# Turning the gated rows of two SwiGLU blocks with transposing DMAs instead of TensorE

## The chip, the cores and the metric

The kernel runs on one core of a Trainium2 chip. The metric is the device time of one execution in microseconds. The core's engines each take their instructions in order: TensorE (PE in the profile; its weight loads are PEld), VectorE (DVE), ScalarE (ACT), GpSimd (POOL) and SyncE (SP). An engine that meets an instruction whose input is not there waits, and everything behind it on that engine waits too. DMAs are issued by SP, ACT or POOL and run on 16 DMA engines that all of them share.

## The reference

A decoder layer on 256 tokens with 2048 channels, all in 32-bit floats. The part that the change touches is the SwiGLU block, which occurs twice (in the kernel f1 and f2), each with 5632 hidden channels:

```
def swiglu(x, w_gate, w_up, w_down):
    return (jax.nn.silu(x @ w_gate) * (x @ w_up)) @ w_down

h = h + 0.5 * swiglu(rmsnorm(h, g_ffn1[l]), w1_gate[l], w1_up[l], w1_down[l])
```

Between the two blocks stand a mixer (a gated spatial unit and a windowed attention) and a cross-attention to a memory; a final RMS norm ends the layer.

## The kernel before, in words

**Matrix products.** Each product of two 32-bit matrices is made of three passes of a faster TensorE format. An operand is split into a high part, which ScalarE makes by a cast (L146, tiles ending in h), and a low part, which VectorE makes by subtracting the high part from the original (L147, tiles ending in l). The passes are high by high, low by high and high by low. On top of that, chunks of one kind (S) take seven products of quarter matrices instead of eight, as Strassen and Winograd do, which needs sums of weights: VectorE makes them in three additions (L319, L322, L323, tile t), and ScalarE and VectorE split them too (th, tl). Chunks of kind C and N need no such sums.

**Streaming.** Weights come in chunks of 1 MB, issued by SP into three buffers (f1gw). The split results gwh and gwl have two buffers, the split sums th and tl one. So ScalarE can cast a chunk's weights as soon as TensorE has finished with the chunk two before, and VectorE subtracts behind it.

**The units.** The gate and up projections are made in 11 units per block, 22 in all. A unit is 512 hidden channels, 8 chunks, and takes about 42 us. At its end VectorE puts the seven products together, ScalarE takes the sigmoid-weighted gate (L671, twice, for the two blocks of 128 tokens) and VectorE multiplies gate and up (L675, twice). The results, called the gated rows, are two tiles of 128 tokens by 512 channels, gp and gz (sg in the very first unit).

**Turning.** The down projection contracts over the hidden channels, so the gated rows must be turned: channels to partitions. rows_done (L655) does it. Its generator turns the rows with eight TensorE transposes of 128x128 per unit, by the identity (L230), four into one PSUM bank; ScalarE copies each bank out into the tile a (L665). These pieces of work are laid between the matmuls of the next unit: side_step counts groups of six matmuls, and the generator asks to go on five groups later and then two groups later. When a tile of a is there, acts holds it, and inner (L681) splits it, for the down projection only, long after.

**What sets the order.** TensorE's order is the program's. The other engines' order is chosen by a scheduler when the program is built. The list later holds functions that are called a given number of chunks after they are put in: an entry with 0 is called in the same chunk step, with 2 two steps later.

Of the kernel before, what the change touches and what calls it, by code (L numbers as in the profile page):

```python
# [7 lines left out]

F32 = mybir.dt.float32
F32R = mybir.dt.float32r  # L10
AF = mybir.ActivationFunctionType
ALU = mybir.AluOpType
AX = mybir.AxisListType

P = 128
T = 256
TB = 2
# [15 lines left out]
def layer_kernel(  # L33
# [22 lines left out]
    nc = tc.nc  # L56
# [13 lines left out]
    def nm(s):  # L70
        uid[0] += 1
        return f"{s}_{uid[0]}"

    def m4(s):
        return mid.tile([P, 1024], F32, tag="m4", name=nm(s))

    def s2(s):
        return tmp.tile([P, 512], F32, tag="s2", name=nm(s))

    def bank(s):  # L80
        return trp.tile([P, 512], F32, tag="tr", name=nm(s))
# [8 lines left out]
    def silu_table():  # L90
        t = tiny.tile([P, 1], F32, tag="warmed", name=nm("warmed"))
        return nc.scalar.activation(t, ones[:, :1], AF.Silu)

# [24 lines left out]
    h = const.tile([P, TB, D], F32, name="h")  # L118
# [15 lines left out]
    def square_into(parts_ap, src, width):  # L134
        junk = s2("junk")
        nc.scalar.activation(junk[:, :width], src, AF.Square, accum_out=parts_ap)

    def split_scaled(hi, lo, src, g):

        nc.scalar.activation(hi, src, AF.Copy, scale=g)  # L140
        nc.vector.scalar_tensor_tensor(
# [27 lines left out]
    def form(s):  # L169
        return [fp.tile([P, 4, P], F32R, tag=t, name=nm(s + t)) for t in ("fh", "fl")]  # L170

    class Pair:
        def __init__(self, s, kind, base=None):
            self.kind = kind
            self.base = base or form(s)
            if kind in "SD":
                self.sums = form(s)
                if kind == "D":
                    self.more = [
                        const.tile([P, 2, P], F32R, tag="more" + t, name=nm(s + "more")) for t in "hl"  # L180
                    ]
# [40 lines left out]
    def laid(kind, k, tb):  # L222
        return BASE[kind].index(f"A{tb + 1}{k + 1}")

    def transposed(s, kind, src):

        ps = bank(s).rearrange("p (k t) -> p k t", k=4)
        for k in range(2):
            for tb in range(TB):
                nc.tensor.transpose(ps[:, laid(kind, k, tb), :], src(tb, k), ident)  # L230
        return ps

    def row_tile(kind, v, k):

        return v[:, k::2, :] if kind == "C" else v[:, 2 * k:2 * k + 2, :]

    def pair_from_rows(s, kind, src, gcol):
# [4 lines left out]
        for k in range(2):  # L242
# [4 lines left out]
            else:  # L247
                nc.scalar.activation(row_tile(kind, raw, k), row_tile(kind, ps, k), AF.Copy, scale=g)
        if kind != "N":
# [60 lines left out]
    def load(s, w, kind, pieces, between):  # L310

        raw = stream.tile([P, 4, 512], F32, tag="raw", name=nm(s + "w"), bufs=3)
        wh = stream.tile([P, 4, 512], F32R, tag="wh", name=nm(s + "wh"))
        wl = stream.tile([P, 4, 512], F32R, tag="wl", name=nm(s + "wl"))
        b = {name: (wh[:, i, :], wl[:, i, :]) for name, i in SLOT.items()}
        if kind == "S":
# [9 lines left out]
            for i, names in enumerate((("T1", "T3"), ("T2", "T4"))):  # L326
                th, tl = [
                    stream.tile([P, 2, 512], F32R, tag=f"{n}{i}", name=nm(s + n), bufs=1)
                    for n in ("th", "tl")
# [93 lines left out]
    def side_add(gen):  # L423
        side.append([now[0], gen])
# [33 lines left out]
    later = []  # L458
# [55 lines left out]
    def narrow_unit(s, w, pairs, late, beside):  # L514

        ps = []
        for c in range(2):
            raw = stream.tile([P, 8, 256], F32, tag="raw", name=nm(s + "w"), bufs=3)
            wh = stream.tile([P, 8, 256], F32R, tag="wh", name=nm(s + "wh"))
            wl = stream.tile([P, 8, 256], F32R, tag="wl", name=nm(s + "wl"))  # L520
# [33 lines left out]
    KINDS_D = "NNSNSNSN" + "NSNSNSN" + "NNSNSNN"  # L554
# [41 lines left out]
    def adds(s, c, j0, on_block=None):  # L596
# [10 lines left out]
        def early(u):  # L607
            p1, v, z = s2(s + "p1"), s2(s + "v"), s2(s + "z")
            nc.scalar.activation(p1, u["P1"], AF.Copy, scale=c)
            nc.vector.scalar_tensor_tensor(  # L610
# [40 lines left out]
    def ffn(s, get, rs, wgu, wd, on_block, first=None, on_token_block=None):  # L651
        acts = [None] * 22
        pairs = [None] * 22

        def rows_done(c, rows_):  # L655
            a = m4(s + "a").rearrange("p (q k t) -> p q k t", q=2, k=4)

            def work():
                for q in range(2):
                    yield 5 if q == 0 else 2  # L660
                    ps = transposed(
                        s + "a", KINDS_D[2 * c + q],
                        lambda tb, k: rows_[tb][:, (2 * q + k) * P:(2 * q + k + 1) * P],
                    )
                    nc.scalar.copy(a[:, q], ps)  # L665
                    acts[2 * c + q] = a[:, q]

            side_add(work())

        def gated(up, sg, r, tb):  # L670
            nc.scalar.activation(  # L671
                sg[1], sg[0], AF.Silu, scale=1.0 if r is None else r[:, tb:tb + 1]
            )
# [13 lines left out]
        def gu_unit(c):  # L687
            got = {}

            def late(u):  # L690
                r = rs()
                c22 = s2(s + "u")
                at = {(0, 0): got["p1"], (1, 1): c22, (0, 1): got["v"], (1, 0): got["z"]}
                seven_late(u, got, lambda tb, j: at[tb, j])
                gated(at[0, 1], (at[0, 0], at[0, 0]), r, 0)
                gated(c22, (at[1, 0], at[1, 0]), r, 1)
                rows_done(c, (at[0, 0], at[1, 0]))

            kinds = MORE if 2 <= c <= 9 else FEWER
            order = range(8)  # L700
            if c == (first is not None):
                order = ORDER[first is None]
            u = Unit(s + "g", "".join(kinds[j] for j in order))
            for i in range(8):
                push(
                    u, i, wgu[order[i], c], lambda j=order[i]: get(j),
                    lambda i=i: (
                        i == u.kinds.rindex("S") and seven_early(u, got), i == 7 and late(u)
                    ),
                    beside=lambda i: (  # L710
                        first[2](8 + i) if first is not None and c == 1
                        else rs() if (c, i) == (0, 5) else inner(i - 5) if c == 10 and i >= 5 else None
                    ),
                )

        def plain_gu_unit(c):
            pairs_, before, prep, rs0 = first
            u = Unit(s + "g", "N" * 8, alone=(7,))
            u.gate_first = True

            def late():
                r = rs0()
                sg = [s2(s + "sg") for _ in range(TB)]
                for tb, (g, up) in enumerate((("P2", "Q3"), ("Q4", "R"))):
                    gated(u[up], (u[g], sg[tb]), r, tb)
                rows_done(c, sg)

            pieces = {0: (1, 0, 3, 2), 1: (1, 3, 0, 2)}
            for i in range(8):
                push(  # L730
                    u, i, wgu[i, c], lambda i=i: have(pairs_, i), late if i == 7 else None,
                    pieces=pieces.get(i), beside=prep, before=before,
                )
# [747 lines left out]
```

## Time and profile before

| what | value |
|---|---|
| median of 3 runs | 2049.84 us (2049.66 to 2049.85) |
| span of the profiled execution | 2047.2 us |
| PE busy | 2034.8 us, 99% |
| DVE busy | 1859.5 us, 91% |
| ACT busy | 1225.4 us, 60% |
| DMA, mean | 196 GB/s |
| granted TensorE clock | 0.999 |

The span runs from the first to the last instruction of one profiled execution; the runs' median is 2.6 us more than it, and that difference is taken as fixed. Busy time of an engine counts its instructions, not its DMA issues. A row of the timeline view gives start, duration, engine, line, output and input tile, and in brackets the idle time before it and what ended it.

### The profile page before, as it was taken

What the parts mean: (1) busy time and instruction counts of PE and PEld (TensorE: products, weight loads), DVE (VectorE), ACT (ScalarE), POOL (GpSimd) and SP (SyncE); (2) the same over time, 40 slices, a digit from 0 to 9 for tenths busy, and PEclk for the clock granted to TensorE, in tenths of its full rate; (3) what the DMA queues carried; (4) which work ended last, traced back from release to release, by engine and by line L of the source; (5) the groups of instructions that cost most, each with busy time, mean ns of one, the idle gap of its engine ahead of it and who ended that gap; (6) DMA issues with size and microseconds to landing.
All of it is one profiled execution on the core that took longest, in us unless ns stands there. A gap on an engine that the chain in (4) does not pass through costs nothing.

```text
span 2047.2 us, 24505 instructions
## 1 busy us (share of the span) xinstructions
PE 2034.8 (99%) x9411; PEld 1690.0 (83%) x9411; DVE 1859.5 (91%) x1998; ACT 1225.4 (60%) x1344; POOL 36.6 (2%) x57
## 2 busy tenths in 40 slices
PE   9999999999999999999999999999999999999998
PEld 7888888888888888888888888888888888888886
DVE  6999999999998978988988977899999999999988
ACT  7755555565555766655556665675555556565554
POOL 0000000000000110100000000000000000000000
PEclk9999999999999999999999999999999999999999
DMA  8555555555555565545545544455455555555563
GB/s 312 182 207 204 206 206 185 205 209 192 203 204 203 188 241 178 195 162 185 202 169 186 204 150 155 171 195 214 185 206 202 205 193 206 202 203 209 185 224 126
DMA packets 60421, 402.21 MB, mean 196 GB/s; under 512 B 6912, under 2 KB 8976, under 8 KB 13200
## 3 DMA queue, kind: packets, MB, share of 16 engines
q1 hardware_dynamic: 57856, 393.50, 53.0%
q0 software_dynamic: 2016, 6.30, 0.9%
q8 instruction: 74, 1.21, 0.2%
q10 hardware_dynamic: 432, 0.84, 0.1%
q14 instruction: 43, 0.35, 0.1%
HBM read 398.52 MB, written 2.10 MB: 196 GB/s over the span
## 4 chain that ended last, share of the span: by engine, by line
PE 97%; DVE 1%; ACT 1%; issue 0%; DMA 0%; POOL 0%; POOLq 0%; DVEq 0%; SPq 0%
PE f1gQ L410 16%; PE f2gQ L410 15%; PE f2dQ L410 6%; PE f1dQ L410 6%; PE f1gP L410 6%; PE f2gP L410 6%; PE xqQ L410 3%; PE f2dP L410 3%; PE f1dP L410 3%; PE woQ L410 2%; PE xoQ L410 2%; PE f2dR L410 2%; PE f1dR L410 2%; PE vQ L410 2%; PE mv0Q L410 2%; PE mv1Q L410 2%
## 5 line engine op out<-in xcount | busy, mean ns | idle before, releaser
L147 DVE TENSOR_TENSOR f1gwl<-f1gw,f1gwh 128x1536 fp32r<-128x1536 f32 (+2 forms) x94 | 181.7, 1935 | 19.8 <-ACT f1gwh L146 16.0
L146 ACT CAST f2gwh<-f2gw 128x1536 fp32r<-128x1536 f32 (+1 forms) x88 | 150.7, 1712 | 69.0 <-PE f2gQ L410 45.5
L146 ACT CAST f1gwh<-f1gw 128x1536 fp32r<-128x1536 f32 (+2 forms) x94 | 153.0, 1629 | 59.9 <-PE f1gQ L410 39.0
L147 DVE TENSOR_TENSOR f2gwl<-f2gw,f2gwh 128x1536 fp32r<-128x1536 f32 (+1 forms) x88 | 179.4, 2039 | 9.5 <-ACT f2gwh L146 7.8
L146 ACT CAST f2gth<-f2gt 128x1024 fp32r<-128x1024 f32 x82 | 84.9, 1050 | 75.9 <-DVE f2gt L319 28.8
L146 ACT CAST f1gth<-f1gt 128x1024 fp32r<-128x1024 f32 x76 | 79.0, 1051 | 76.1 <-DVE f1gt L319 30.1
L410 PE MATMUL f2gQ<-f2gwh,n4fh 128*128 128x512 f32 x317 | 124.5, 393 | 0.0
L410 PE MATMUL f2gQ<-f2gwh,n4fl 128*128 128x512 f32 x317 | 123.4, 389 | 0.0
L146 ACT CAST f2dwh<-f2dw 128x2048 fp32r<-128x2048 f32 (+1 forms) x44 | 77.3, 1757 | 61.6 <-PE f2dQ L410 39.6
L410 PE MATMUL f1gQ<-f1gwh,n1fh 128*128 128x512 f32 x286 | 112.4, 393 | 0.0
L410 PE MATMUL f1gQ<-f1gwh,n1fl 128*128 128x512 f32 x286 | 111.3, 389 | 0.0
L146 ACT CAST f1dwh<-f1dw 128x2048 fp32r<-128x2048 f32 (+1 forms) x44 | 77.3, 1758 | 56.6 <-PE f1dQ L410 38.1
L147 DVE TENSOR_TENSOR f2gtl<-f2gt,f2gth 128x1024 fp32r<-128x1024 f32 x82 | 99.6, 1220 | 8.9 <-ACT f2gth L146 8.4
L147 DVE TENSOR_TENSOR f1dwl<-f1dw,f1dwh 128x2048 fp32r<-128x2048 f32 (+1 forms) x44 | 92.1, 2093 | 12.6 <-ACT f1dwh L146 12.5
L147 DVE TENSOR_TENSOR f2dwl<-f2dw,f2dwh 128x2048 fp32r<-128x2048 f32 (+1 forms) x44 | 92.1, 2094 | 11.5 <-ACT f2dwh L146 11.3
L147 DVE TENSOR_TENSOR f1gtl<-f1gt,f1gth 128x1024 fp32r<-128x1024 f32 x76 | 92.4, 1220 | 7.7 <-ACT f1gth L146 7.2
L410 PE MATMUL f2gQ<-f2gwl,n4fh 128*128 128x512 f32 x317 | 97.6, 392 | 0.0
L410 PE MATMUL f1gQ<-f1gwl,n1fh 128*128 128x512 f32 x286 | 88.0, 393 | 0.0
L410 PEld LDWEIGHTS f2gQ<-f2gwh,n4fh 128*128 128x128 f32 x317 | 59.5, 188 | 12.3 <-DVE f2gv L569 0.4
L410 PEld LDWEIGHTS f2gQ<-f2gwh,n4fl 128*128 128x128 f32 x317 | 59.5, 188 | 11.9
L410 PE MATMUL f2gP<-f2gwh,n4fh 128*128 128x512 f32 x176 | 68.8, 391 | 0.0
L410 PEld LDWEIGHTS f2gQ<-f2gwl,n4fh 128*128 128x128 f32 x317 | 58.8, 188 | 12.0
(828 smaller groups left out, 6045.8 us busy)
## 6 DMA issues: line engine op xcount, KB each, us to landing
f2gw<-in_w_gu SPq DMA_DIRECT2D x88, 1024.0 KB, 4.8
f1gw<-in_w_gu SPq DMA_DIRECT2D x86, 1024.0 KB, 4.9
f1dw<-in_w_down SPq DMA_DIRECT2D x44, 1024.0 KB, 4.8
f2dw<-in_w_down SPq DMA_DIRECT2D x44, 1024.0 KB, 4.8
wow<-in_w_out SPq DMA_DIRECT2D x16, 1024.0 KB, 4.8
xqw<-in_w_xq SPq DMA_DIRECT2D x16, 1024.0 KB, 4.8
xow<-in_w_xo SPq DMA_DIRECT2D x16, 1024.0 KB, 4.8
qw<-in_w_in SPq DMA_DIRECT2D x8, 1024.0 KB, 4.8
```

The costliest lines, as they stand in the source:

```text
L146: nc.scalar.copy(hi, src)
L147: nc.vector.tensor_tensor(lo, src, hi.bitcast(F32), ALU.subtract)
L410: nc.tensor.matmul(self.banks[name], x, y, start=name not in self.begun, stop=self.left[name] == 0)
```

## The change

The eight transposes and two copies of each unit go. In their place, each of the two row tiles (512 words of 32 bits in each partition) is seen as 1024 halves of 16 bits. ScalarE copies the halves into a new tile w, first all low halves, then all high halves, two runs without gaps (L664 of the changed kernel, two per unit). ScalarE's queue then issues a transposing DMA from w to a tile t (L669, two per unit): eight blocks of 128x128 of 16 bits, each turned. Four ScalarE copies (L677) put the halves together again as 32-bit words in the tile a, two of them for each tile t. The function turned (parting and issuing) is called in the chunk step in which the rows are finished, joined (the four copies) two steps later. The new tiles w and t are taken from the same pool of six buffers (s2) from which gp, gz and the other row tiles come.

```diff
         def rows_done(c, rows_):
-            a = m4(s + "a").rearrange("p (q k t) -> p q k t", q=2, k=4)
-
-            def work():
+            a = m4(s + "a")
+            words = a.bitcast(U16).rearrange("p (q i t h) -> p q i t h", q=2, i=4, h=2)
+            halves_ = []
+
+            def turned():
+                for tb in range(TB):
+                    w = s2(s + "w").bitcast(U16)
+                    nc.scalar.copy(
+                        w.rearrange("p (h c) -> p h c", h=2),
+                        rows_[tb].bitcast(U16).rearrange("p (c h) -> p h c", h=2),
+                    )
+                    t = s2(s + "t").bitcast(U16)
+                    nc.scalar.dma_start_transpose(t.rearrange("p (b r) -> p b r", b=8), w)
+                    halves_.append(t.rearrange("p (h b t) -> p b t h", h=2, b=4))
+
+            def joined():
                 for q in range(2):
-                    yield 5 if q == 0 else 2
-                    ps = transposed(
-                        s + "a", KINDS_D[2 * c + q],
-                        lambda tb, k: rows_[tb][:, (2 * q + k) * P:(2 * q + k + 1) * P],
+                    kind = KINDS_D[2 * c + q]
+                    for tb in range(TB):
+                        i, j = laid(kind, 0, tb), laid(kind, 1, tb)
+                        nc.scalar.copy(
+                            words[:, q, i:j + 1:j - i], halves_[tb][:, 2 * q:2 * q + 2]
+                        )
+                    acts[2 * c + q] = a[:, q * 512:(q + 1) * 512].rearrange(
+                        "p (k t) -> p k t", k=4
                     )
-                    nc.scalar.copy(a[:, q], ps)
-                    acts[2 * c + q] = a[:, q]
-
-            side_add(work())
+
+            later.append((0, turned))
+            later.append((2, joined))
```

Lines of the changed kernel are 1 later than those of the kernel before ahead of rows_done and 17 later behind it.

**Where the instructions now stand.** On ScalarE, in the kernel before, the stretch from the second gate function of the seventh unit of f1 (f1gz) on. L146 casts weights (gwh) and sums of weights (gth); L665 empties the two banks of turned rows:

```order
L671 ACTIVATE f1gp_460_2459<-f1gp_460_2459 128x512
L146 CAST f1gwh_2519<-f1gw_2518 128x2048
L671 ACTIVATE f1gz_2461<-f1gz_2461 128x512
L146 CAST f1gwh_2553<-f1gw_2552 128x1536
L146 CAST f1gth_2562<-f1gt_2556 128x1024
L146 CAST f1gwh_2601<-f1gw_2600 128x2048
L665 COPY f1a_2517<-f1a_2588 128x512
L146 CAST f1gth_2566<-f1gt_2556 128x1024
L665 COPY f1a_2517<-f1a_2612 128x512
L146 CAST f1gwh_2634<-f1gw_2633 128x1536
```

The two copies stand apart, each between casts. In the changed kernel the same stretch, from the cast behind that gate function on, where L664 parts a row tile, L669 issues its transposing DMA and L677 joins:

```order
L147 CAST f1gwh_2527<-f1gw_2526 128x2048
L688 ACTIVATE f1gz_2461<-f1gz_2461 128x512
L147 CAST f1gwh_2561<-f1gw_2560 128x1536
L664 COPY f1w_2518<-f1gp_472_2459 128x1024
L669 DMA_TRANSPOSE f1t_2520<-f1w_2518 128x8x128
L664 COPY f1w_2522<-f1gz_2461 128x1024
L669 DMA_TRANSPOSE f1t_2524<-f1w_2522 128x8x128
L677 COPY f1a_2517<-f1t_2520 128x2x256
L147 CAST f1gth_2570<-f1gt_2564 128x1024
L677 COPY f1a_2517<-f1t_2520 128x2x256
L677 COPY f1a_2517<-f1t_2524 128x2x256 x2
L147 CAST f1gwh_2607<-f1gw_2606 128x2048
```

All parting, issuing and joining of the unit now stands in one block, with a single cast (gth) in it, between the cast of the next S chunk's weights and the cast of the chunk after it.

On VectorE, in the kernel before, the same place: L675 finishes the gated rows, L319 to L323 add weights, and L147 makes the low parts:

```order
L147 TENSOR_TENSOR f1gwl_2520<-f1gw_2518,f1gwh_2519 128x2048
L675 TENSOR_TENSOR f1gp_460_2459<-f1gv_2460,f1gp_460_2459 128x512
L675 TENSOR_TENSOR f1gz_2461<-f1u_2507,f1gz_2461 128x512
L319 TENSOR_TENSOR f1gt_2556<-f1gw_2552 128x1024
L147 TENSOR_TENSOR f1gwl_2554<-f1gw_2552,f1gwh_2553 128x1536
L322 TENSOR_TENSOR f1gt_2556<-f1gt_2556,f1gw_2552 128x512
L147 TENSOR_TENSOR f1gtl_2563<-f1gt_2556,f1gth_2562 128x1024
L323 TENSOR_TENSOR f1gt_2556<-f1gt_2556,f1gw_2552 128x512
L147 TENSOR_TENSOR f1gwl_2602<-f1gw_2600,f1gwh_2601 128x2048
L147 TENSOR_TENSOR f1gtl_2567<-f1gt_2556,f1gth_2566 128x1024
```

And in the changed kernel:

```order
L692 TENSOR_TENSOR f1gp_472_2459<-f1gv_2460,f1gp_472_2459 128x512
L692 TENSOR_TENSOR f1gz_2461<-f1u_2507,f1gz_2461 128x512
L148 TENSOR_TENSOR f1gwl_2528<-f1gw_2526,f1gwh_2527 128x2048
L320 TENSOR_TENSOR f1gt_2564<-f1gw_2560 128x1024
L148 TENSOR_TENSOR f1gwl_2562<-f1gw_2560,f1gwh_2561 128x1536
L323 TENSOR_TENSOR f1gt_2564<-f1gt_2564,f1gw_2560 128x512
L148 TENSOR_TENSOR f1gtl_2571<-f1gt_2564,f1gth_2570 128x1024
L324 TENSOR_TENSOR f1gt_2564<-f1gt_2564,f1gw_2560 128x512
L148 TENSOR_TENSOR f1gwl_2608<-f1gw_2606,f1gwh_2607 128x2048
L148 TENSOR_TENSOR f1gtl_2575<-f1gt_2564,f1gth_2574 128x1024
```

VectorE has the same work. The two products that finish the gated rows (L692 here) have moved ahead of one low part of 2048 columns; the rows behind it are in the same order. The last four of them, gtl, an addition, gwl and gtl, need the casts gth, gwh and gth that stand in and behind ScalarE's block.

1 line of the change is left out of this document (added).

## The prediction

> **What bounds the kernel now.** I read the page first: its span, the shares of the engines, and the chain that ended last.
>
> ```profile
> span 2047.2 us, 24505 instructions
> PE 2034.8 (99%) x9411; PEld 1690.0 (83%) x9411; DVE 1859.5 (91%) x1998; ACT 1225.4 (60%) x1344; POOL 36.6 (2%) x57
> PE 97%; DVE 1%; ACT 1%; issue 0%; DMA 0%; POOL 0%; POOLq 0%; DVEq 0%; SPq 0%
> ```
>
> TensorE bounds the whole. Whatever leaves its stream is time, if nothing else holds it up. Then I read stretches of 42 us, the length of one unit, in f1 and in f2:
>
> ```profile
> core 0: us, PE busy (x) PEld busy (x) DVE busy (x) ACT busy (x) POOL busy (x), PEclk, DMA share, GB/s
> 274.00:316.00 42.00, 42.00 (x190) 34.76 (x189) 40.26 (x39) 24.38 (x22) 0.00 (x0) 1.00 0.55 200
> 1572.00:1614.00 42.00, 42.00 (x190) 34.76 (x189) 40.39 (x38) 24.45 (x22) 0.00 (x0) 1.00 0.55 204
> ```
>
> This is where the change sits, and 91% is the wrong number here: VectorE is busy 40.3 of 42 us, and has 1.7 us to lose. ScalarE has 17.6 us free, but it is the engine that feeds both.
>
> **What leaves TensorE.** In the chain of waits, between 300 and 325 us, one unit's eight transposes are two pieces:
>
> ```profile
> 314.81 0.44 PE f1a L230 x4
> 318.01 0.43 PE f1a L230 x4
> ```
>
> 0.87 us a unit, on the chain. (The 272 ns that a transpose lasts overlap with its neighbours and are not its price.) 22 units make 19.1 us; that is all that can be won, and the profiled execution would become 2028.
>
> **What ScalarE gets.** Its timeline at the end of f1's seventh unit and in the one that follows:
>
> ```profile
> 297.66 1.48 ACT L146 CAST f1gwh<-f1gw 128x1536 fp32r<-128x1536 f32 x1 [0.59 <-PE f1gQ L410]
> 299.05 1.99 ACT L146 CAST f1gth<-f1gt 128x1024 fp32r<-128x1024 f32 x2
> 307.63 0.63 ACT L671 ACTIVATE f1gz<-f1gz 128x512 f32<-128x512 f32 x1
> 308.16 1.47 ACT L146 CAST f1gwh<-f1gw 128x1536 fp32r<-128x1536 f32 x1
> 312.51 1.06 ACT L146 CAST f1gth<-f1gt 128x1024 fp32r<-128x1024 f32 x1 [2.88 <-DVE f1gt L319]
> 314.43 1.91 ACT L146 CAST f1gwh<-f1gw 128x2048 fp32r<-128x2048 f32 x1 [0.86 <-PE f1gQ L410]
> 316.25 0.58 ACT L665 COPY f1a<-f1a 128x512 f32<-128x512 f32 x1
> 316.72 1.06 ACT L146 CAST f1gth<-f1gt 128x1024 fp32r<-128x1024 f32 x1
> 318.49 0.59 ACT L665 COPY f1a<-f1a 128x512 f32<-128x512 f32 x1 [0.71 <-PE f1a L230]
> ```
>
> Two copies go, 1.17 us. Two partings of 1024 elements come, and four joins of 512. A 16-bit copy is not in this trace; the nearest rows are the cast of 1024 (1.06 us) and the copy of 512 (0.58 us; the next instruction starts after 0.47), and I take these. Bounds: half of it, if an element of half the size takes half the time; twice the parting, if reading every second half costs double. Issue of a DMA by ScalarE, and the time from issue to landing, stand in these rows:
>
> ```profile
> L1400 ACTq DMA_DIRECT2D out<-hg x2: 344/351/358, 2038.8 to 2041.6; - x2
> out<-hg ACTq DMA_DIRECT2D x1, 256.0 KB, 3.2
> mr<-in_mem POOLq DMA_DIRECT2D x8, 256.0 KB, 5.3
> sm<-in_small ACTq DMA_DIRECT2D x1, 52.0 KB, 2.5
> h<-in_x SPq DMA_DIRECT2D x4, 512.0 KB, 10.9
> ```
>
> An issue takes 0.35 us. **The landing time L of a transposing DMA of 256 KB is the unknown of this forecast.** Of the two plain 256 KB transfers the one at the kernel's end, with no load of weights beside it, took 3.2 us, the other, beside such loads, 5.3. The DMA engines are 55% busy here, so I take the middle, 4.25 us. Below, 2.5 us (the smallest transfer on this queue); above, 10.9 us, the slowest row, for the case that eight blocks are turned one after another.
>
> The Trainium skill states two things that disagree. "Advanced Engine Details and Errata", X-Bar Transpose (TRN2), says that transposing DMAs are as fast as plain ones, 350 to 400 GB/s; with the fixed 2.0 us of "DMA: Bandwidth & Descriptors", Anatomy of one DMA, that is an estimate of 2.75 us, and the sum below would give 2059. "VectorE: DVE Perf Modes", The three transpose paths, gives 1309 ns for one 128x128 block by DMA and advises TensorE where PSUM will do; eight blocks in a row would be an estimate of 10.5 us, and 2206. No run here shows which holds yet.
>
> **Where it lands in the program.** Parting, issuing and joining stand in one block on ScalarE behind the cast of 308.16, as the order shows, and the join of the first tile waits for its landing with the casts gth, gwh and gth queued behind it. By the rows above: first parting 309.55 (1.39 behind the cast's start, as from 297.66 to 299.05) to 310.60, issue at 310.60; second parting 310.95 to 312.0, issue to 312.35. First join at 310.60 + L, 314.85 with L = 4.25. Then, at the distances of the trace (0.47 a join, as from 316.25 to 316.72; 0.95 the cast, since two in a row take 1.99 with the overlap), gth at 315.32, a join at 316.27, and the second tile's two at 316.74 and 317.21 (landed at 316.25). The cast gwh starts at 317.68, not 314.43: **late by L - 1.0, 3.25 us**. In general it is the first join, not ScalarE's own work, that sets this as long as L is over 1.75.
>
> **Who waits for it.** VectorE, and then TensorE:
>
> ```profile
> 314.59 1.22 DVE L147 TENSOR_TENSOR f1gtl<-f1gt,f1gth 128x1024 fp32r<-128x1024 f32 x1
> 315.73 0.69 DVE L323 TENSOR_TENSOR f1gt<-f1gt,f1gw 128x512 f32<-128x512 f32 x1
> 316.72 2.29 DVE L147 TENSOR_TENSOR f1gwl<-f1gw,f1gwh 128x2048 fp32r<-128x2048 f32 x1 [0.31 <-ACT f1gwh L146]
> 318.93 1.22 DVE L147 TENSOR_TENSOR f1gtl<-f1gt,f1gth 128x1024 fp32r<-128x1024 f32 x1
> 320.60 0.39 PE L410 MATMUL f1gQ<-f1gth,n1fl 128*128 128x512 f32 x1
> 320.83 1.07 PE L410 MATMUL f1gQ<-f1gtl,n1fh 128*128 128x512 f32 x4
> ```
>
> VectorE's gwl already starts right behind the cast (0.31 idle), and the second gtl right behind gwl. So both move by the same 3.25 us: the second gtl ends at 323.40, not 320.15. TensorE reads it in the third of the four matmuls that begin at 320.83, at 321.28 (a matmul starts every 0.227 us). The slack was 1.13 us. The four transposes of 314.81 and those of 318.01 fall away ahead of that matmul, so it only comes earlier; their 0.87 us is won and lost in the same wait. Per unit the change is
>
> lateness - slack = (L - 1.0) - 1.13 = L - 2.13, at L = 4.25: **+2.12 us**.
>
> VectorE's own account agrees: it can lose 1.7 us a unit; 40.3 of work, with the two new waits ahead of gtl and gwl, 1.8 us each by the same rows, come to 43.9 instead of 41.9.
>
> **The sum.** The chunk order that this rests on (an S chunk, then a C chunk) follows 8 units of each block, 16 in all. The other 6, at the blocks' ends, stand ahead of chunks without that tight gtl; they lie between -0.87 and +2.12, and I take the middle, +0.62. Together 16 x 2.12 + 6 x 0.62 = 37.6 us. In general 19 x (L - 2.13) - 2.6. On the profiled execution 2047.2 becomes 2084.8; on the median, 2.6 us above it, 2049.8 becomes **2088**. With parting at twice the time, 1.05 us more a unit, 2108.
>
> Costed at nothing: the fewer PSUM banks, since no transpose waited for one; the tiles w and t from a pool of six, since each is freed by the joins long before the next unit's rows are made (without that cover the next unit's first copy out of P1 would wait for the joins); and 0.5 MB of transposes beside 8 MB of weights a unit, which SP issues ahead of use into three buffers (if the DMA engines were held for long, the casts would wait for weights).
>
> **The rivals.**
>
> *A transposing DMA lands as a plain one does*, L = 3.2: 19 x 1.07 - 2.6 = +18, **2068**. For it: the same bytes, and the row of this very queue. Against it: that row had the DMA engines to itself. The Trainium skill's first rule is on this side.
>
> *Block after block*, L = 10.9: 19 x 8.77 - 2.6 = +164, **2214**. For it only that 16 bits are moved one by one instead of rows of kilobytes; no row shows it. The Trainium skill's second rule is on this side.
>
> *Faster: the block on ScalarE is short enough.* It wins where the cast gwh is late by less than the slack of 1.13 us; there the wait turns into a part of the 0.87 us. With 16-bit copies at half the time and L = 3.2, the first parting ends at 310.10, the first join starts at 313.30, and gwh at 315.25: late by 0.82, -0.31 a unit. With full copies and a landing that is over before the second issue is, joins start at 312.35 and gwh at 315.18: late by 0.75, -0.38 a unit. With 16 such units and 6 halfway to -0.87 that is -8.5 to -10 us, **2040**. Both at once would win the 19 us, 2031. For it: ScalarE is idle 17.6 of 42 us. Against it: the smallest transfer on its queue needs 2.5 us, and L must be under 2.27 to break even at full copies.
>
> That the transposes stay on TensorE is excluded: none of the 176 stands in its new order.
>
> **How the numbers follow.** My forecast, a landing of 3.6 to 6.5 us, has 0.44 (2075 to 2130 by the formula); the plain landing, 2.4 to 3.6 us (2052 to 2075), 0.21; block after block 0.13; the faster rival 0.22. The time is that of the forecast, 2088. The range takes in the faster rival's two simple forms at 2040 and reaches to a landing of 6.7 us, 19 x 4.57 - 2.6 = +84, 2135 rounded up; what it leaves out is most of the slow case and the best of the faster one. A measurement of this kernel tells 0.2%, 4.1 us, from no change. Of the faster rival 0.18 lies beyond that and 0.04 within, and of the plain landing 0.02 within: faster 0.18, same 0.06, slower 0.76.
>
> **What would show it.** In the changed profile, waits of L677 for a DMA of 1 to 4 us in nearly every unit; the cast gwh behind it 2 to 4 us later against the second gate function; VectorE idle ahead of gtl and gwl for casts; TensorE's idle before matmuls that read gtl, about 2 us a unit, where it had none; a unit of 44 us instead of 41.9. Wrong is the forecast if L677 does not wait, or if it waits and TensorE still has no idle time, because the slack of one chunk was larger than this one unit shows; wrong in size if the issue itself holds ScalarE for microseconds, or if TensorE waits for weights instead.

## The result

The changed kernel takes **2142.62 us** (2141.70 to 2143.80), the kernel before, on the same chip, 2049.76 us: a ratio of 1.0454, with a 95% interval of 1.0441 to 1.0467. It is slower, by 92.9 us. The forecast was 2088 us with a range of 2040 to 2135; the direction was right, and the size was less than half of what came.

The page of the changed kernel, its span and the shares of the engines:

```profile
span 2140.6 us, 24260 instructions
PE 2061.3 (96%) x9235; PEld 1698.1 (79%) x9235; DVE 1860.9 (87%) x1998; ACT 1294.7 (60%) x1432; POOL 34.4 (2%) x57
```

The 176 transposes are gone (9411 to 9235 instructions on TensorE), and yet TensorE is busy 26.5 us longer than before. The span grew by 93.4 us, and these rows split it: TensorE's idle time went from 12.4 us (2047.2 less 2034.8) to 79.3 (2140.6 less 2061.3), which is 66.9 of it; its busy time gives the other 26.5.

Who waits for whom (total us, times, longest), from the view of waits of the changed kernel:

```profile
DVE f1gwl L148 <- ACT f1gwh L147: 68.9, 27, 5.2
...
ACT f1a L677 <- DMA f1t<-f1w: 36.6, 17, 3.9
ACT f2a L677 <- DMA f2t<-f2w: 33.1, 16, 2.9
...
PE f1gQ L411 <- ACT f1gth L147: 31.7, 8, 4.8
...
PE f2gQ L411 <- ACT f2gth L147: 28.5, 7, 4.7
```

The joins wait for the landing; behind them the casts are late, VectorE waits for the cast gwh, and in 15 units, 8 in f1 and 7 in f2, TensorE waits for the cast gth for about 4 us. One such place, on ScalarE:

```profile
291.48 1.47 ACT L147 CAST f1gwh<-f1gw 128x1536 fp32r<-128x1536 f32 x1
292.85 1.04 ACT L664 COPY f1w<-f1gp 128x1024 uint16<-128x1024 uint16 x1
293.92 1.25 ACTq L669 DMA_TRANSPOSE f1t<-f1w  x1
295.21 1.05 ACT L664 COPY f1w<-f1gz 128x1024 uint16<-128x1024 uint16 x1 [1.32 <-issue]
296.29 1.25 ACTq L669 DMA_TRANSPOSE f1t<-f1w  x1
297.58 0.68 ACT L677 COPY f1a<-f1t 128x512 uint16<-128x512 uint16 x1 [1.32 <-DMA f1t<-f1w]
298.17 1.05 ACT L147 CAST f1gth<-f1gt 128x1024 fp32r<-128x1024 f32 x1
299.11 0.68 ACT L677 COPY f1a<-f1t 128x512 uint16<-128x512 uint16 x1
302.12 1.25 ACT L677 COPY f1a<-f1t 128x512 uint16<-128x512 uint16 x2 [2.33 <-DMA f1t<-f1w]
303.28 1.89 ACT L147 CAST f1gwh<-f1gw 128x2048 fp32r<-128x2048 f32 x1
305.08 1.04 ACT L147 CAST f1gth<-f1gt 128x1024 fp32r<-128x1024 f32 x1
```

This is the block that the prediction laid out, with the joins' waits in it (rows of a queue, such as ACTq, are issues). The issue of one DMA holds ScalarE for 1.25 us, the second tile lands 5.8 us after its issue (296.29 to 302.12), and the cast gwh starts 11.80 us after the cast of 1536 columns that leads the block, where it was 6.27 before (308.16 to 314.43). What TensorE does meanwhile:

```profile
302.04 0.39 PE L411 MATMUL f1gQ<-f1gth,n1fl 128*128 128x512 f32 x1
306.17 0.79 PE L411 MATMUL f1gQ<-f1gth,n1fh 128*128 128x512 f32 x1 [3.74 <-ACT f1gth L147]
306.76 0.63 PE L411 MATMUL f1gQ<-f1gth,n1fl 128*128 128x512 f32 x1
307.19 0.63 PE L411 MATMUL f1gQ<-f1gth,n1fh 128*128 128x512 f32 x1
```

It waits 3.74 us, and then its matmuls start 0.43 us apart instead of 0.227. The granted clock says why; stretches of the same execution (PE busy, weight loads, DVE, ACT, POOL, granted clock, DMA share, GB/s):

```profile
305.10:311.90 6.80, 5.73 (x14) 4.35 (x15) 6.66 (x5) 2.75 (x4) 0.00 (x0) 0.50 0.50 177
311.90:352.80 40.90, 38.07 (x168) 31.16 (x166) 33.47 (x33) 24.41 (x23) 0.00 (x0) 1.00 0.60 188
```

**After each of the 15 long waits the clock stands at half for 6.8 us.** In the first of these stretches TensorE was busy 5.73 us for work that needs 2.87 at the full clock. The trace's record of the clock has 15 such stretches, all of 6.83 us; 15 x 2.87 is 43 us. Before, none is in it. (Every kernel's record ends with one more stretch, which begins behind TensorE's last matmul and costs nothing; it is left out here and below.) Another row gives nearly the same: the kernel without the DMAs (no_dma, below) runs the same 9235 instructions of TensorE without a long wait, and its TensorE is busy 2017.3 us; 2061.3 less that is 44.0. So the 93.4 us are +66.9 of idle time, +44.0 of matmuls (some 43 of it at half clock), and -17.5 for the transposes that are gone (2017.3 less 2034.8).

"TensorE: Matmul & The Clock Gate" of the Trainium skill (What's actually happening) says that TensorE falls to half its clock after at least one idle window of about 3.4 us and comes back after a busy one. The halving is in the rows above, and the lengths agree: 6.83 us is two such windows. But no window here had to be idle from end to end, as the trace's record of the clock shows.

**What halves the clock.** In the change the slow stretches begin at 113.93, 161.72 and so on to 448.44 us in f1, and at 1540.70 in f2: 1426.77 us after the first, which is 418 times 3.4133 us. All 51 slow stretches, in the change and the six kernels below that have any, begin on such a grid of fixed moments, one for each execution, to within 5 ns. Cut along it, TensorE's busy time separates all cases: the clock fell after every 3.41-us window at full clock in which TensorE was idle for 1.83 us or more, and after none with less, in all 14 traces. (The least idle time that a fall followed is 1.832 us, the most that none followed 1.828.) It came back after the first window at half clock with less than 0.50 us of idle time. Three windows of the grid, the first two from the change, the third from one_more_copy below (columns as above):

```profile
301.67:305.08 3.41, 0.76 (x4) 0.30 (x2) 0.00 (x0) 2.96 (x3) 0.00 (x0) 1.00 0.81 259
1496.33:1499.74 3.41, 1.60 (x7) 1.32 (x8) 1.62 (x1) 3.41 (x3) 0.00 (x0) 1.00 0.12 50
```

```profile
538.01:541.42 3.41, 1.47 (x8) 0.89 (x6) 1.85 (x4) 3.41 (x5) 0.00 (x0) 1.00 0.29 118
```

The first, with 2.65 us idle, ends where the stretch at half clock above begins, 1.1 us before the wait is over. The second holds nearly all of a wait of 1.89 us, 1.81 us of idle time, and no slow stretch follows; the third holds a whole wait of 1.94 us, and one does.

### The profile page after: what moved, and what is told of

It reads as the page before. It is cut to its first block, busy times and chain, and to the rows that moved or that the text cites. A ratio compares the mean times of both kernels' runs of the same rounds, so it can differ in the third digit from the quotient of the medians.

```text
span 2140.6 us, 24260 instructions
## 1 busy us (share of the span) xinstructions
PE 2061.3 (96%) x9235; PEld 1698.1 (79%) x9235; DVE 1860.9 (87%) x1998; ACT 1294.7 (60%) x1432; POOL 34.4 (2%) x57
## 5 line engine op out<-in xcount | busy, mean ns | idle before, releaser
L147 ACT CAST f1gwh<-f1gw 128x1536 fp32r<-128x1536 f32 (+2 forms) x94 | 152.6, 1625 | 47.4 <-PE f1gQ L411 24.0
L147 ACT CAST f2gwh<-f2gw 128x1536 fp32r<-128x1536 f32 (+1 forms) x88 | 150.0, 1708 | 44.8 <-PE f2gQ L411 28.0
L147 ACT CAST f2gth<-f2gt 128x1024 fp32r<-128x1024 f32 x82 | 85.7, 1050 | 93.3 <-DVE f2gt L320 56.3
L147 ACT CAST f1gth<-f1gt 128x1024 fp32r<-128x1024 f32 x76 | 79.7, 1051 | 90.3 <-DVE f1gt L320 60.6
L147 ACT CAST f2dwh<-f2dw 128x2048 fp32r<-128x2048 f32 (+1 forms) x44 | 77.3, 1757 | 59.2 <-PE f2dQ L411 41.7
L147 ACT CAST f1dwh<-f1dw 128x2048 fp32r<-128x2048 f32 (+1 forms) x44 | 77.2, 1755 | 51.1 <-PE f1dQ L411 33.1
L411 PE MATMUL f2gQ<-f2gth,n4fh 128*128 128x512 f32 x164 | 68.3, 417 | 28.5 <-ACT f2gth L147 28.5
L411 PE MATMUL f1gQ<-f1gth,n1fh 128*128 128x512 f32 x152 | 64.4, 424 | 31.9 <-ACT f1gth L147 31.7
```

What stands on the lines that cost most here:

```text
L147: nc.scalar.copy(hi, src)
L411: nc.tensor.matmul(self.banks[name], x, y, start=name not in self.begun, stop=self.left[name] == 0)
```

## The experiments

Each kernel is the changed one with the edit shown; each ratio is to the kernel before on the same chip, which took 2049.1 to 2049.4 us.

### Taking the DMAs away, and taking only the wait for them away

no_dma leaves the transposing DMAs out and joins the parted rows unturned:

```diff
-                    t = s2(s + "t").bitcast(U16)
-                    nc.scalar.dma_start_transpose(t.rearrange("p (b r) -> p b r", b=8), w)
-                    halves_.append(t.rearrange("p (h b t) -> p b t h", h=2, b=4))
+                    halves_.append(w.rearrange("p (h b t) -> p b t h", h=2, b=4))
```

> As the run whose joins don't wait, and without the DMAs: ScalarE only parts and joins (the down projections get rows that are not turned). Theory: partings and joins together put the second gth cast where it was before, 8.5 us behind the cast of the S chunk's weights; no idle, no half clock: 2031 us, 2028 to 2040; the difference to the run with unawaited DMAs is the price of two issues of 1.25 us. Rival (3.3 us more copying a unit on ScalarE are themselves too much for a VectorE that is 96% busy): over 2055.

Measured: 2033.91 us, 0.9924 (0.9909 to 0.9939). The shares of its engines, from its page:

```profile
PE 2017.3 (99%) x9235; PEld 1672.3 (82%) x9235; DVE 1859.0 (91%) x1998; ACT 1292.9 (64%) x1432; POOL 34.3 (2%) x57
```

TensorE's busy time is the 2017.3 us used above, and it has no wait over 2.2 us. joins_dont_wait keeps both DMAs on ScalarE's queue, but its joins read w, so nobody waits for the landing (rows unturned again):

```diff
-                    halves_.append(t.rearrange("p (h b t) -> p b t h", h=2, b=4))
+                    halves_.append(w.rearrange("p (h b t) -> p b t h", h=2, b=4))
```

> The changed kernel, but the joins read the parted tile w instead of the turned tile t: the DMAs are issued and run, nobody waits for their landing (the down projections get rows that are not turned). Theory (the landing of the second DMA, 5.8 us behind its issue in the unit looked at, is the larger part of the lateness): second gth cast 2.5 us later than in the kernel before instead of 5.0, TensorE idle 1.3 us a unit, shorter than what halves the clock, 2040 to 2065 us. Rival (the issue hold and the copies alone do it): idle of 3 us or more a unit stays, clock 0.50 in nearly every unit, over 2110.

Measured: 2062.60 us, 1.0065 (1.0050 to 1.0080). So the steps from before to the change are -15.2 us for partings and joins in place of TensorE's transposes, +28.7 for having the DMAs issued by ScalarE, and +80.0 for waiting for their landing. They are not quite pure, because the scheduler's order is not the same in the three kernels. On ScalarE all four joins stand ahead of the cast gth in no_dma, and only one of them in the other two, in joins_dont_wait even ahead of the second issue; VectorE's order is the same in nearly all units of f1, but in f2 no_dma has another. Of joins_dont_wait, ScalarE's timeline behind the second issue, and TensorE's waits:

```profile
276.32 1.25 ACTq L669 DMA_TRANSPOSE f1t<-f1w  x1
277.66 1.05 ACT L147 CAST f1gth<-f1gt 128x1024 fp32r<-128x1024 f32 x1 [0.78 <-ACT f1a L677]
```

```profile
PE f2gQ L411 <- ACT f2gth L147: 6.3, 5, 2.4
PE f1gQ L411 <- ACT f1gth L147: 5.6, 7, 0.8
```

The cast gth waits for ScalarE's own issue to be over. The profile names the copy ahead of the issue as what ended its wait, but that copy had long been done. The waits of TensorE are mostly under 1 us, those for gtl (12.2 us in all) included, and the clock stays up: the one wait of 2.42 us was followed by the only slow stretch, of 3.41 us.

### Moving the issue to SyncE's queue alone

sp_alone:

```diff
-                    nc.scalar.dma_start_transpose(t.rearrange("p (b r) -> p b r", b=8), w)
+                    nc.sync.dma_start_transpose(t.rearrange("p (b r) -> p b r", b=8), w)
```

> The changed kernel with its transposing DMAs issued from SP, and the joins where the scheduler puts them, ahead of the casts. Theory: two holds of 1.25 us fall away, the wait for the second landing stays; the second gth cast is about 3.8 us late instead of 5.0, TensorE's idle 2.6 us a unit, too short to halve the clock; 2060 to 2090 us, few or no slow stretches. Rival (the length of the idle does not decide on the clock): slow stretches in nearly every unit and over 2100.

Measured: 2053.59 us, 1.0026 (1.0015 to 1.0036), below what was expected. The issuing queue is the whole edit, and 89 us are gone. The waits of ScalarE's joins, and TensorE's longest:

```profile
ACT f1a L677 <- DMA f1t<-f1w: 20.1, 9, 3.8
...
ACT f2a L677 <- DMA f2t<-f2w: 9.9, 9, 1.2
```

```profile
PE f1gQ L411 <- ACT f1gth L147: 8.8, 8, 2.4
```

The joins still wait, 30.0 us instead of 69.7, but TensorE's longest wait for a gth is 2.4 us, and there are two slow stretches instead of 15 (in the profiled execution, which at 2058.4 us was the slowest of seven). The one edit changes two things: ScalarE is no longer held, and the landing is sooner (median 3.2 us, in the change 3.5 and 4.3); this run doesn't part them. Still, neither waiting for the landing alone nor the issue on ScalarE alone makes the 93 us. Together they bring TensorE's wait to about 4 us, and there each wait has 2.9 us of slow matmuls behind it.

### A plain DMA in its place

plain_dma moves w to t by a plain DMA on the same queue; the rows aren't turned:

```diff
-                    nc.scalar.dma_start_transpose(t.rearrange("p (b r) -> p b r", b=8), w)
+                    nc.scalar.dma_start(t, w)
```

> The changed kernel with a plain DMA from w to t in place of the transposing one, from the same queue (the down projections get rows that are not turned). If a transposing DMA is as fast as a plain one: the same idle times, the same clock, over 2120 us. If the transposing itself costs (issue 1.25 instead of 0.35 us, landing 3.5 to 5.8 instead of some 3.2): idle of about 1 us a unit, no slow stretch, 2040 to 2065 us.

Measured: 2111.52 us, 1.0302 (1.0275 to 1.0330; two runs, 12 us apart), between the two outcomes expected, so neither was right. The time from issue to landing (last number, median us), first of plain_dma, then of the change:

```profile
f1t<-f1w ACTq DMA_DIRECT2D x22, 256.0 KB, 2.5
f2t<-f2w ACTq DMA_DIRECT2D x22, 256.0 KB, 2.4
```

```profile
f1t<-f1w ACTq DMA_TRANSPOSE x22, 3.5
f2t<-f2w ACTq DMA_TRANSPOSE x22, 4.3
```

The plain copy lands 1 to 2 us sooner and its issue takes 0.47 us instead of 1.25. TensorE's waits shrink from about 4 us to between 2.9 and 3.8, and that does not get it out of the trap: 14 waits, 13 slow stretches, nine of 6.83 us and four of 3.41. A wait of 3 us is long enough for the half clock here.

### A later cast in the same trap

one_more_copy puts one more copy of 512 columns on ScalarE ahead of the joins:

```diff
+                nc.scalar.copy(s2(s + "x"), rows_[1])
```

> The changed kernel with one more ScalarE copy of 512 words behind the second issue, whose result nobody reads; by the order, three joins instead of two now stand behind the landing of the second DMA, so the second gth cast starts about 0.57 us later. Theory that the units are locked to the clock gate (15 units of 47.79 us, of which 6.83 at half clock: an idle time that ends later leaves less of the slow stretch to work in): less than half of it comes through, 2140 to 2147 us, the same number of slow stretches, the same distance of 47.79 us between them. Rival (no lock; each unit gets longer by its idle time): +0.57 us in some 16 units, 2152 us.

Measured: 2148.38 us, 1.0486 (1.0468 to 1.0503), 5.8 us above the change, in neither of the two places expected. In f1 the units are as long as in the change: TensorE's eight waits are longer, 4.43 us each on the mean instead of 3.96, but from the first to the last are 334.75 us, as against 334.21 in the change, and the slow stretches start 47.79 us apart in both. What a wait gains in length, the slow stretch loses in work done at half clock: it begins before the wait is over (by 1.1 us in the rows above) and its end stays where it was. In f2 the distance is not so regular (some gaps are 44.37 us and some stretches 3.41), and two waits of 1.8 and 1.9 us in the down projections, each followed by 3.41 us at half clock, are new; there are 18 slow stretches in all. 47.79 us is 14 times 3.413, the distance of the fixed moments. That the fixed moments hold the units to this length fits all this: a wait that ends later leaves less work to the slow stretch, which ends when it would have ended anyway. That it is why the units lock is argued, not shown.

### Taking the joins out of the way

The scheduler had moved the joins right behind the issues, though joined is called two chunks later. joins_in_order holds them in program order, four chunks later:

```diff
-                        nc.scalar.copy(
+                        tc.keep_in_program_order(nc.scalar.copy(
...
-            later.append((2, joined))
+            later.append((4, joined))
```

> The changed kernel, with the four joins held back by two more chunk steps and pinned on ScalarE behind what the program has put there by then, so that the casts gth, gwh and gth stand ahead of them; nothing is left out. Theory (the casts behind the waiting joins make TensorE idle, and each such idle time of about 4 us is followed by 6.8 us at half clock): by the changed kernel's own rows the second gth cast would start 0.2 us later against the gate function than in the kernel before, within its slack; no idle time of TensorE over 1 us, no stretch at clock 0.50, and the whole gain of the transposes is kept: 2031 us, 2028 to 2042. Rival (ScalarE's added work and the two issues of 1.25 us are the cause, not the place of the joins): still over 2100. Rival (the transposing DMAs slow the weights or the clock by themselves): still over 2090, with TensorE waiting for other things than gth.

Measured: 2052.59 us, 1.0016 (1.0007 to 1.0026). The joins no longer wait and the clock stays up, which is 90 us of the 93. But 2031 was expected, and it is not even faster than before. order_and_sp adds SyncE's queue to it:

```diff
-                    nc.scalar.dma_start_transpose(t.rearrange("p (b r) -> p b r", b=8), w)
+                    nc.sync.dma_start_transpose(t.rearrange("p (b r) -> p b r", b=8), w)
```

> As the run with the joins pinned behind the casts, and the two transposing DMAs issued from SP's queue instead of ScalarE's; nothing is left out. Theory: what that run still lost against the run without DMAs (2052.6 to 2033.9) is the 1.25 us that each of 44 issues holds ScalarE; on SP, which has seconds to spare between loads into three buffers, it costs nothing: 2030 to 2037 us, TensorE's waits for gtl gone, clock 1.00 throughout. Rival (the transposing transfers themselves slow what runs beside them): 2045 to 2055, with waits for weights or longer casts.

Measured: 2053.97 us, 1.0023 (1.0013 to 1.0032): a miss, ScalarE's issues are not the cause here. joins_on_gpsimd gives the change's joins to GpSimd:

```diff
-                        nc.scalar.copy(
+                        nc.gpsimd.tensor_copy(
```

> The changed kernel with the four joins on GpSimd instead of ScalarE; nothing is left out. Theory: the casts stand behind nothing that waits; left are the partings and the two issue holds on ScalarE, so about the run with pinned joins: 2040 to 2055 us, no slow stretch. Rival (GpSimd's copies disturb VectorE, which works on the same memory): VectorE's instructions get longer, over 2060.

Measured: 2062.31 us, 1.0063 (1.0047 to 1.0078): not the 2040 to 2055 of the theory but the rival, over 2060 with longer instructions of VectorE. A join takes GpSimd three times as long, and VectorE's own work is slower beside it (gtl 1.30 us instead of 1.22). Busy us and mean ns of one, and the idle time ahead:

```profile
L677 POOL COPY f2a<-f2t 128x512 uint16<-128x512 uint16 x44 | 94.0, 2172 | 384.1 <-DMA f2t<-f2w 351.2 <-PE f2gQ L411 32.8
...
L148 DVE TENSOR_TENSOR f1gtl<-f1gt,f1gth 128x1024 fp32r<-128x1024 f32 x76 | 98.8, 1303 | 2.3 <-ACT f1gth L147 1.7
```

### The missing 20 us: the DMAs, or the order

Two causes were left for the 20 us between these kernels and no_dma: the DMAs' traffic and landing, or the order that the scheduler writes once the joins are four chunks later. no_dma_order4 has that order without the DMAs (rows unturned); against joins_in_order:

```diff
-                    t = s2(s + "t").bitcast(U16)
-                    nc.scalar.dma_start_transpose(t.rearrange("p (b r) -> p b r", b=8), w)
-                    halves_.append(t.rearrange("p (h b t) -> p b t h", h=2, b=4))
+                    halves_.append(w.rearrange("p (h b t) -> p b t h", h=2, b=4))
```

> The order of joins_in_order (joins four chunks later and held in program order) without any transposing DMA: the joins read w. It leaves out the transposes, so its rows aren't turned. Open is why joins_in_order and order_and_sp stayed near 2053 where no_dma is at 2034. Theory O: with joins four chunks later the scheduler writes another order around the gates (VectorE's gtl behind both gate products), which alone costs the 20 us: 2049 to 2056, with TensorE waiting some 15 us in all for gtl. Theory D: the DMAs themselves cost it, by traffic or by the landing: 2031 to 2037 and no wait for gtl.

Measured: 2053.20 us, 1.0020 (1.0011 to 1.0030). **It is the order.** Without any DMA all of the loss is there, and so are the waits for gtl. VectorE at a unit's end in no_dma_order4, TensorE there, and TensorE's waits:

```profile
268.58 0.68 DVE L690 TENSOR_TENSOR f1gp<-f1gv,f1gp 128x512 f32<-128x512 f32 x1
269.18 1.22 DVE L148 TENSOR_TENSOR f1gtl<-f1gt,f1gth 128x1024 fp32r<-128x1024 f32 x1
270.32 0.68 DVE L690 TENSOR_TENSOR f1gz<-f1u,f1gz 128x512 f32<-128x512 f32 x1
270.92 1.22 DVE L148 TENSOR_TENSOR f1gtl<-f1gt,f1gth 128x1024 fp32r<-128x1024 f32 x1
```

```profile
270.45 0.50 PE L411 MATMUL f1gQ<-f1gtl,n1fh 128*128 128x512 f32 x1 [0.94 <-DVE f1gtl L148]
```

```profile
PE f2gQ L411 <- DVE f2gtl L148: 7.2, 13, 1.0
PE f1gQ L411 <- DVE f1gtl L148: 7.0, 9, 0.9
```

And VectorE at the same place in no_dma:

```profile
261.43 1.21 DVE L148 TENSOR_TENSOR f1gtl<-f1gt,f1gth 128x1024 fp32r<-128x1024 f32 x1
262.56 0.68 DVE L569 TENSOR_TENSOR f1u<-f1gQ,f1gz 128x512 f32<-128x512 f32 x1
...
264.96 1.21 DVE L148 TENSOR_TENSOR f1gtl<-f1gt,f1gth 128x1024 fp32r<-128x1024 f32 x1
266.09 0.68 DVE L690 TENSOR_TENSOR f1gp<-f1gv,f1gp 128x512 f32<-128x512 f32 x1
```

In no_dma the two gtl stand within the work on the seven products, ahead of the gate products (L690 in both kernels); in no_dma_order4 the first stands behind one gate product and the second behind both, and TensorE waits 0.94 us for the first in this unit. order_and_sp has the same order and waits of 7.3 and 7.1 us. The waits shown make 14.2 of the 19 us. TensorE's busy time is 5.4 us longer too (2022.6 against 2017.3), at full clock; the cause of that is not traced. ScalarE's order differs between the two kernels as well, so it is the new order as a whole that costs the 19 us.

The last three hold the joins at other counts; the edit shown is against the change. order6_and_sp:

```diff
-                    nc.scalar.dma_start_transpose(t.rearrange("p (b r) -> p b r", b=8), w)
+                    nc.sync.dma_start_transpose(t.rearrange("p (b r) -> p b r", b=8), w)
...
-                        nc.scalar.copy(
+                        tc.keep_in_program_order(nc.scalar.copy(
...
-            later.append((2, joined))
+            later.append((6, joined))
```

> Joins six chunks later, where the scheduler leaves VectorE's gate section nearly as in no_dma, and the transposing DMAs on SyncE's queue. Theory O: 2031 to 2038, no wait of TensorE for gtl above 2 us in all; faster than before. Theory D: 2048 to 2056, as order_and_sp.

Measured: 2039.04 us, 0.9950 (0.9935 to 0.9965). It is faster than before and close to the expected range, not in it; TensorE's waits for gtl are 1.5 us in f1 (7.3 with the other order), and 1.5 us for gwl are new. order6_on_act is the same with ScalarE issuing, as in the change:

> As order6_and_sp, but with the DMAs issued by ScalarE, as in the change: this adds only the two issues of 1.25 us a unit to ScalarE. In no_dma ScalarE ran a block of 4.5 us (two partings, four joins) at this place without harm; two partings and two issues take 4.6 us. If that carries over: 2031 to 2040. If the issue harms beyond its length, or O is wrong: 2045 to 2065.

Measured: 2041.58 us, 0.9966 (0.9953 to 0.9979), just beyond the expected 2040. Here 44 issues of 1.25 us on ScalarE cost 2.5 us in all; the same issues cost 28.7 between no_dma and joins_dont_wait, where the joins stand right behind them. order3_and_sp is order6_and_sp with a count of 3:

> Joins three chunks later, held in program order, DMAs on SyncE's queue. On ScalarE a cast gth, a cast gwh and their waits stand between the second parting and the first join, about 3 us, where the landing took 3.1; three joins (1.9 us) then stand ahead of the next gth. If the landing is just over: 2034 to 2045. If the joins still wait for it (over 0.5 us in most units): 2045 to 2070, with waits of TensorE for gth or gtl.

Measured: **2033.64 us, 0.9923 (0.9906 to 0.9939)**, the fastest kernel that turns the rows, 0.4 us under the expected 2034 to 2045, 15.6 us faster than before and level with no_dma. ScalarE from a parting to the joins, the DMAs' landing, and a stretch of one unit's length:

```profile
269.44 1.04 ACT L664 COPY f1w<-f1gz 128x1024 uint16<-128x1024 uint16 x1
272.27 1.06 ACT L147 CAST f1gth<-f1gt 128x1024 fp32r<-128x1024 f32 x1 [1.79 <-DVE f1gt L320]
273.38 1.92 ACT L147 CAST f1gwh<-f1gw 128x2048 fp32r<-128x2048 f32 x1
275.20 1.84 ACT L677 COPY f1a<-f1t 128x512 uint16<-128x512 uint16 x3
```

```profile
f1t<-f1w SPq DMA_TRANSPOSE x22, 3.2
```

```profile
274.00:316.00 42.00, 42.00 (x185) 34.25 (x185) 40.78 (x39) 27.99 (x26) 0.00 (x0) 1.00 0.63 214
```

The landing of 3.2 us passes under ScalarE's idle 1.79 us and two casts that it has to do anyway; the joins wait 0.2 us in the whole kernel, and TensorE has no idle time in the stretch. No part of the change is left out here, so the gain is to be had with the rows turned by DMA.

## Why the prediction came out as it did

**What was right.** The place and the chain: the block on ScalarE in the order laid out, the joins' wait (L677) for the landing with gth and gwh queued behind it, VectorE idle ahead of gwl, TensorE idle once a unit. The gain was nearly right, 19.1 us predicted, 15.2 (no_dma) and 15.6 (order3_and_sp) measured once nothing is in its way. The unknown on which the forecast rested, a landing of 4.25 us, was well placed: medians 3.5 and 4.3, range 3.0 to 7.4. That was partly luck: it was the middle of two rows of plain DMAs, and a plain copy in this very place landed in 2.4 to 2.5. Parting took 1.04 us, where 1.06 was taken.

**The step that failed is the price of TensorE's wait**: "Per unit the change is lateness - slack". That step counts a wait at its own length. A wait of the size that the prediction itself foresaw, 2.12 us and the 0.87 won, so 3.0 us, was already followed by half the clock in plain_dma, and in the change each of the 15 was. This term was not in the sum at all; the trace has 43 to 44 us of it. The forecast was +37.6 in all, so its TensorE idle time is +56.7 (37.6 and the 19.1 of gain); measured was +66.9. As the trace has it, the miss on the spans, 93.4 less 37.6, is 44.0 of clock, 10.2 of idle time, and 1.6 of a gain of 17.5 instead of 19.1.

The two causes are more nearly equal than that, for the half clock hides a second wait. In the unit shown TensorE goes on at 306.17, and the second gtl ends 2.46 us later:

```profile
307.42 1.22 DVE L148 TENSOR_TENSOR f1gtl<-f1gt,f1gth 128x1024 fp32r<-128x1024 f32 x1
```

Six matmuls stand ahead of the one that reads it. At full clock they would have taken 1.36 us (6 x 0.227), and TensorE would have waited 1.1 us more. The trace has the same 1.1 us in all 15 units, 16.5 us. So without the half clock, as an estimate, the idle time would have been about 83 us, 27 more than forecast, and the clock by itself costs some 27 us, not 44.

**The lateness was too small as well.** An issue was taken as 0.35 us from the row of the output's DMA and holds ScalarE for 1.25; a join took 0.68 us, not 0.58; and the second tile was to land 0.49 us ahead of its first join (316.25 and 316.74), but in the unit shown it lands 5.8 us after its issue, and the join waits 2.33 us for it. In that unit gwh was 5.53 us late against the 3.25 foreseen; the first join came 6.10 us after the start of the leading cast, ahead of the 6.69 foreseen. "Wrong in size if the issue itself holds ScalarE for microseconds" had been named, and it did.

**The waiter was another, with the same cause.** The prediction had TensorE wait for the second gtl. It waits for the second gth: gth is 5.04 us late (305.08 - 291.48 against 316.72 - 308.16) and had 2.13 us of slack (it ended at 317.78 before, and the matmul that first reads it, below, began at 319.91), and with the transposes' 0.87 that gives 3.78 of wait, where 3.74 stand in the rows. The four matmuls behind it then run at half clock, 306.17 to 308.04, and only so does gtl, which is late too, come in time for its own. TensorE before:

```profile
319.91 0.39 PE L410 MATMUL f1gQ<-f1gth,n1fh 128*128 128x512 f32 x1
```

**The unit.** 41.9 - 0.87 + 3.96 of wait (the mean in f1) + 2.87 of slow matmuls is 47.86; the distance in the trace is 47.79. The forecast was 44.

**The rivals.** Block after block (2214) is out: it needs 10.9 us for each landing, and the longest of the change's 44 took 7.4. The plain landing (2068) is out too: on the same queue and place a plain copy landed in 2.4 to 2.5 us, and the transposing one 1.0 to 1.9 us later. By these rows the Trainium skill's "as fast as regular DMAs" ("Advanced Engine Details and Errata", X-Bar Transpose (TRN2)) does not hold for this tile's landing; from SyncE's queue it took 3.2 us, nearer to the plain copy's 2.5 but still 0.7 more. The fixed 2.0 us that the prediction adds stands in its section of the Trainium skill ("DMA: Bandwidth & Descriptors", Anatomy of one DMA) for DMAs that GpSimd issues; these are issued by ScalarE. The faster case (2040) did not come with the change, but its condition, gwh late by less than the slack, is what order3_and_sp, order6_and_sp and order6_on_act bring about (in nearly all units of f1, gwh is 0.0, 0.0 and about 0.85 us late there by the same reckoning), and they took 2034 to 2042.

**What stays open.** Whether the fixed moments of the clock are what locks the units to 47.79 us, and why in one_more_copy they do so in f1 and not fully in f2; no run set TensorE's waits against those moments on purpose. And why transposing DMAs from ScalarE's queue land later than from SyncE's: medians of 3.3 to 5.1 us for f1 and f2 in the six kernels that issue there, 3.1 to 3.2 in the four that use SyncE's.

## What to carry to other kernels

Price a wait on TensorE at its own length only if it is short: here a window of 3.41 us with 1.83 us or more of idle time was followed by 3.4 or 6.8 us at half clock, so a small saving in the chain (an issue moved to another queue) was worth 89 us, and a delay of 0.47 us a unit nothing in f1. Before counting the slow matmuls in full, look for a wait that they hide. Put the consumer of a DMA where the engine has other work for longer than the landing takes, and hold it there if a scheduler would pull it forward. After moving one group of instructions, read the order of the other engines again: here four copies held elsewhere on ScalarE changed VectorE's order too, and the new order, without any DMA, cost 19 us.

## What the runs showed of the hardware

- TensorE's granted clock changed only at fixed moments 3.413 us apart (51 slow stretches in seven kernels, to within 5 ns). It fell to 0.50 after each window at full clock in which TensorE was idle for 1.83 us or more (by the trace's matmul records, whose ends are modelled), and after no window with less; it came back after a window with less than 0.50 us of idle time.
- So the length of a wait decides only in part. In the change the clock stood at 0.50 for 6.83 us with each wait of 3.5 to 4.8 us, in plain_dma for 3.41 or 6.83 us with 13 of 14 waits of 2.9 to 3.8 us. Of the 13 waits of 1.8 to 2.5 us in all kernels, 8 were followed by a slow stretch (the shortest 1.83 us, in one_more_copy) and 5 were not (the longest 2.18 us, in no_dma). "TensorE: Matmul & The Clock Gate" of the Trainium skill (Why this matters for your kernels) advises against idle gaps over about 3 us; by these rows harm can begin lower, at 1.8 us.
- The issue of one transposing DMA of 128x1024 halves of 16 bits held ScalarE for 1.25 us; a plain one of the same bytes 0.47.
- Beside loads of weights, a transposing DMA landed 3.0 to 7.4 us after its issue in the change (up to 11.4 in joins_on_gpsimd), a plain copy of the same tile 2.2 to 6.6 in plain_dma.
- A 16-bit copy with every second element read (L664, 1024 elements) took 1.04 us, as long as a 32-bit cast of 1024 elements; a join, writing every second half, 0.68 us for 512.
